# Block-diagonal products of a delta-rule scan: two half-array matmuls replaced by one matmul over the whole 128x128 array

## The chip, the cores and the metric

The kernel runs on one core of one Trainium2 chip. The metric is the device time of the whole program in microseconds (us), the median of several runs. TensorE has two lanes in the profile: PE is the matmul itself and PEld the load of its stationary operand (the weights). DVE is VectorE, ACT is ScalarE, POOL is GpSimd, SP issues the DMAs. TensorE's granted clock has two levels, 1.2 and 2.4 GHz; a granted clock of 0.92 over a stretch is a mixture of both.

## The reference, cut to what matters

One decoder layer over 2048 tokens: an RWKV-7 token mixer (12 heads of width 64) beside a 4-head cross-attention into 256 memory tokens, an output projection, and a squared-ReLU MLP of width 4096. What the change touches is this recurrence, and two small sums:

```python
def step(S, inp):                                   # one token, S is (heads, 64, 64)
    sa = einsum('bhvk,bhk->bhv', S, a_t)
    S = S * w_t + sa[..., None] * b_t + v_t[..., None] * k_t
    return S, einsum('bhvk,bhk->bhv', S, r_t)
bonus = sum(r_h * k_h * r_k, axis=-1) * v_h         # one number per token and head
q = rms_norm(q_mem)                                 # needs the sum of squares per token and head
```

The kernel computes the recurrence in chunks of 64 tokens. Within a chunk each head needs the inverse of a unit lower triangular 64x64 matrix; between chunks only S is carried.

## The kernel before, in words

**Stages.** First comes an input projection, `project(g)`, for four groups of 512 tokens; its matmuls are line 102 (`pz`). Then 16 pairs of chunks are worked through: `prepare(p)` builds everything of a pair that doesn't depend on S, `scan(d, S)` carries S through the pair's two chunks, and `post(p, ...)` normalises and gates the output. The projections of groups 1 to 3, the memory attention and the output projection (`output(g)`, line 629, `pout`) are spread between the pairs by `dense(...)`, as work for TensorE to do while the pairs wait for their small steps. At the end stands the MLP (lines 964 and 1073), which the change doesn't touch.

**Order.** A planner puts the instructions of each engine in an order, by priorities (`tc.cur_priority`) and by a simulated timeline. Each engine then runs its instructions strictly in that order. Buffers come from pools; a tile with `bufs=1` makes its next user wait until its last reader is done. All PSUM tiles of tag `z` (`psb`, `pb`, `pe`, `pe2`) share one buffer, and an engine that reads a PSUM tile and one that writes it take turns.

**The inverse.** Per chunk, twelve 64x64 matrices are inverted from 32x32 blocks. The two diagonal blocks of all heads come from a loop on DVE (lines 431 and 435) and arrive in the tile Z by DMA (line 447), head q=0 of a pair of heads in partitions 0 to 63 and head q=1 in 64 to 127, both in their own 64 columns; the rest of Z is zero. The off-diagonal block takes two products. Line 453 transposes the upper diagonal block on DVE into `te`. Line 459 multiplies it by the off-diagonal block of `PT`, one matmul per head with 32 weight columns and 32 moving columns, six heads of one q after the other, and line 461 copies the six results to `te2` on ACT. Line 466 multiplies `te2` (32 weight columns) by Z, again six heads at a time, and line 467 copies the six results on ACT into Z's off-diagonal block.

**Its use.** In `scan`, line 491 multiplies Z by the right side `rhs`: per pair of heads two matmuls, with 64 weight columns and 64 moving columns each. Around it, lines 485 (`prhs`) and 498 (`pS`) are products with 64 weight columns too.

**The small norms.** Line 405 (`psb`, for the bonus) and line 761 (`pq`, for the memory attention's query norm) multiply 128 tokens of a product by a matrix of two columns, 64 tokens at a time: 64 weight columns, 2 moving columns.

Each float32 matmul has two records in the profile, each with a weight load of its own. Twelve matmuls are so 24 records.

**Scratch.** `rows_norm` (line 150) writes a squared copy that nobody reads, `junk`, into a buffer of its own.

Of the kernel before, what the change touches and what calls it, by code (L numbers as in the profile page):

```python
# [9 lines left out]
F32 = mybir.dt.float32  # L10
# [9 lines left out]
P = 128  # L20
# [40 lines left out]
def hybrid_layer(  # L61
# [138 lines left out]
    def scan_setup():  # L200
        K["kkc"] = col(rw_k_k[0], "kkc")
        kac = col(rw_k_a[0], "kac")
        K["lbc"] = col(rw_lnx_b[0], "lbc")
        K["ka2"] = ka2 = cb.tile([P, NB], F32, name="ka2")
        nc.vector.tensor_scalar_mul(ka2, kac, 0.5)
        K["ka1"] = ka1 = cb.tile([P, NB], F32, name="ka1")
        nc.vector.tensor_scalar(ka1, kac, -0.5, 1.0, ALU.mult, ALU.add)
        K["lgr"] = lgr = cb.tile([P, MW], F32, name="lgr")
        nc.sync.dma_start(lgr, rw_lnx_g.to_broadcast([P, MW]))

        K["lora"], K["lob"] = [], []
        for which, (w2, w0) in enumerate(((rw_w2, rw_w0), (rw_a2, rw_a0))):
            src = pr.tile([P, MW], F32, tag="kk", name="lsrc")
            for o in range(2):
                nc.sync.dma_start(src[o * HD : (o + 1) * HD], w2[0])
            wt = cb.tile([P, MW], F32R, name=f"lora{which}")
            lo = pr.tile([P, MW], F32R, tag="EM", name="llo")
            nc.scalar.copy(wt[:HD], src[:HD])
            nc.scalar.copy(lo[HD:], src[HD:])
            nc.vector.tensor_tensor(wt[HD:], src[HD:], lo[HD:].bitcast(F32), op=ALU.subtract)  # L220
            K["lora"].append(wt)
            b0 = col(w0[0], f"lob{which}")
            nc.vector.tensor_scalar_mul(b0, b0, 0.5)
            K["lob"].append(b0)

        K["sel2"] = sel2 = cb.tile([96 + NH, MW], BF16, name="sel2")
        nc.gpsimd.memset(sel2, 0.0)
        for o in PARTS:
            so = sel2[o : o + NH]
            nc.gpsimd.memset(so, 1.0)  # L230
            nc.gpsimd.affine_select(so, so, pattern=[[1, MW]], compare_op=ALU.is_ge,
                                    fill=0.0, base=0, channel_multiplier=-HD)
            nc.gpsimd.affine_select(so, so, pattern=[[-1, MW]], compare_op=ALU.is_ge,
                                    fill=0.0, base=HD - 1, channel_multiplier=HD)
        K["rn3"] = rn3 = cb.tile([96 + NH, P], BF16, name="rn3")
        nc.gpsimd.memset(rn3, 0.0)
        K["g2s"] = g2s = cb.tile([P, MW], F32, name="g2s")
        nc.sync.dma_start(g2s, rw_g2[0])
        K["rkm"] = rkm = cb.tile([P, NB, 2], F32, name="rkm")
        nc.vector.memset(rkm, 0.0)  # L240
        rk_src = rw_r_k[0].rearrange("(b two) d -> two d b", two=2)
        nc.sync.dma_start(rkm[:HD, :, 0], rk_src[0])
        nc.sync.dma_start(rkm[HD:, :, 1], rk_src[1])

        K["sel1"] = sel1 = cb.tile([P, NB * NH], F32, name="sel1")
        nc.vector.memset(sel1, 0.0)
        nc.vector.memset(sel1[:HD, 0 : 14 * NB - 13 : 14], 1.0)
        nc.vector.memset(sel1[HD:, 1 : 14 * NB - 12 : 14], 1.0)

        K["msk"] = msk = cb.tile([P, P], F32, name="msk")  # L250
        nc.gpsimd.memset(msk, 1.0)
        nc.gpsimd.affine_select(msk[:HD, :C], msk[:HD, :C], pattern=[[1, C]], compare_op=ALU.is_ge,
                                fill=0.0, base=-1, channel_multiplier=-1)
        nc.gpsimd.affine_select(msk[:HD, C:], msk[:HD, C:], pattern=[[1, C]], compare_op=ALU.is_ge,
                                fill=0.0, base=0, channel_multiplier=-1)
        nc.sync.dma_start(msk[HD:], msk[:HD])
        K["rst"] = rst = cb.tile([P, 2 * P], F32, name="rst")
        nc.vector.memset(rst, 1.0)
        nc.vector.memset(rst.rearrange("p (a c) -> p a c", c=C)[:, :, 0], 0.0)

        zrow = K["zrow"] = dram.tile([2, 512], F32, name="zrow")
        ztmp = pr.tile([1, 512], F32, tag="zt", name="ztmp")
        for par in range(2):
            nc.vector.memset(ztmp, 0.0)
            nc.vector.memset(ztmp[:, par : 512 : 34], 1.0)
            nc.sync.dma_start(zrow[par : par + 1], ztmp)
        K["E"] = cb.tile([P, NB, 2, C + 1], F32, name="E")

        K["Z"] = [cb.tile([P, NB, 2 * C], F32, name=f"Z{i}") for i in range(3)]
        K["te2"] = [cb.tile([P, NB, 32], F32, name=f"te2{i}") for i in range(2)]  # L270
        nc.vector.memset(K["E"][:, :, :, 0], 1.0)
        for t in K["Z"] + K["te2"]:
            nc.gpsimd.memset(t, 0.0)
        S = st.tile([P, NB, HD], F32, tag="S", name="S")
        nc.vector.memset(S, 0.0)
        return S
# [4 lines left out]
    def prepare(p):  # L281
# [118 lines left out]
        nc.vector.tensor_tensor(kp, kp, R, op=ALU.mult)  # L400
        psb = psz.tile([P, NH], F32, tag="z", name="psb")
        for b in range(NB):
            for c in range(2):
                cc = slice(c * C, c * C + C)
                nc.tensor.matmul(psb[cc, 2 * b : 2 * b + 2], kp[:, b, cc], K["rkm"][:, b, :],
                                 start=True, stop=True)
        bs = pr.tile([P, NH], F32, name="bs", bufs=2)
        nc.scalar.copy(bs, psb)
        tc.cur_priority += UPS
# [32 lines left out]
        for c in range(2):  # L442
            d = ch[c]
            d["Z"] = Z = K["Z"][(2 * p + c) % 3]
            for q in range(2):
                for o in (q * C, q * C + 32):
                    nc.sync.dma_start(Z[o : o + 32, :, o : o + 32],
                                      zdr[o // 32 % 2, c, q * NB : (q + 1) * NB].rearrange("i s t -> s i t"))

            te = pr.tile([32, NH, 32], F32, name="te")  # L450
            te2 = K["te2"][c]
            for q in range(2):
                nc.vector.transpose(te[:, q * NB : (q + 1) * NB, :],
                                    Z[q * C : q * C + 32, :, q * C : q * C + 32])
            pe = psz.tile([P, NB, 32], F32, tag="z", name="pe")
            for q in range(2):
                lo = slice(q * C + 32, q * C + C)
                for b in range(NB):
                    nc.tensor.matmul(pe[lo, b, :], d["PT"][:32, q * NB + b, 32:C], te[:, q * NB + b, :],
                                     start=True, stop=True)  # L460
                nc.scalar.copy(te2[lo], pe[lo])
            pe = psz.tile([P, NB, 32], F32, tag="z", name="pe2")
            for q in range(2):
                hi, lo = slice(q * C, q * C + 32), slice(q * C + 32, q * C + C)
                for b in range(NB):
                    nc.tensor.matmul(pe[hi, b, :], te2[:, b, :], Z[:, b, lo], start=True, stop=True)
                nc.scalar.copy(Z[hi, :, lo], pe[hi])

            for q in range(2):
                nc.scalar.copy(d["PT"][:C, q * NB : (q + 1) * NB, :C], d["AR"][q * C : (q + 1) * C, :, :C])  # L470
        return dict(ch=ch, bs=bs)

    def scan(d, S):
        states = []
        for c in range(2):
# [11 lines left out]
            nc.scalar.copy(rhs, pc)  # L487
            pc = psc.tile([P, NB, HD], F32, tag="c", name="pw")
            for b in range(NB):
                for q in range(2):  # L490
                    nc.tensor.matmul(pc[q * C : (q + 1) * C, b, :], Z[:, b, q * C : (q + 1) * C], rhs[:, b, :],
                                     start=True, stop=True)
            for q in range(2):
                nc.scalar.copy(bycol(WV[:C])[:, q], pc[q * C : (q + 1) * C])
            pS = psc.tile([P, NB, HD], F32, tag="c", name="pS")
# [138 lines left out]
    def project(g):  # L634
        xh, xl = operands("xh"), operands("xl")
        for tt in range(4):
            tc.cur_priority -= UPX
            xt = ck.tile([P, D], F32, tag="PT", name="xt", bufs=4) if g == 0 else xrows("xt")
            r0 = g * G + tt * P
            nc.sync.dma_start(xt, x[r0 : r0 + P, :])  # L640
            rows_norm(xp, xt, xt, xp.tile([P, D], BF16, name="junk"))
            tsl = slice(tt * P, (tt + 1) * P)
            for _ in to_T(psx, "x", xt, halves(xh, xl, tsl)):
                tc.cur_priority += UPX
                yield
                tc.cur_priority -= UPX
            tc.cur_priority += UPX
# [63 lines left out]
    def memory_setup():  # L711
# [10 lines left out]
        for mb in range(2):  # L722
            mt = xrows("mt")
            nc.sync.dma_start(mt, mem[mb * P : (mb + 1) * P, :])
            rows_norm(xp, mt, mt, xp.tile([P, D], BF16, name="junk"))
            msl = slice(mb * P, (mb + 1) * P)
            yield from to_T(psx, "x", mt, [(mh[h][:, :, msl], ml[h][:, :, msl]) for h in range(2)])
        for part in range(2):
# [23 lines left out]
    def mem_attention(g, t0):  # L752
# [3 lines left out]
        nc.scalar.activation(qq, q2, AF.Square)  # L756
        pq = psx.tile([P, MH], F32, tag="x", name="pq")
        for b in range(2):
            for c in range(2):
                cc = slice(c * C, c * C + C)  # L760
                nc.tensor.matmul(pq[cc, 2 * b : 2 * b + 2], qq[:, b, cc], sel3, start=True, stop=True)
        yield
        qr = rsqrt_mean(xp, pq, MH, HD, RMS_EPS, "q")
        mxs = xp.tile([P, MH], F32, name="mxs")
# [376 lines left out]
```

## Time and profile before

| | |
|---|---|
| median of three runs | 2777.49 us (2774.64 to 2781.78) |
| the profiled execution's own time | 2781.47 us |
| its span, first to last instruction | 2779.8 us |
| mean granted TensorE clock | 0.956 |
| PE busy | 2620.1 us (94%), 17620 records |
| PEld busy | 2131.9 us (77%) |
| DVE busy | 1807.5 us (65%) |
| ACT busy | 1410.8 us (51%) |
| POOL busy | 413.1 us (15%) |

Busy time is the union of the durations of an engine's instructions. Matmuls are pipelined: one shows about 200 ns or more from start to end, and its successor starts long before that end. What a group of small matmuls costs TensorE is read from the starts: from the group's first start to the start of the next group. A shape such as "128*32 128x32 f32" means 128 rows and 32 weight columns of the array, and a moving operand of 32 columns; the load's own shape stands after PEld.

### The profile page before, as it was taken

How to read it: one execution, taken by the hardware profiler on the slowest of the kernel's cores; microseconds unless marked ns; L12 is line 12 of the kernel's file. 1: busy time of each engine (PE TensorE's matmuls, PEld its weight loads, DVE VectorE, ACT ScalarE, POOL GpSimd, SP SyncE). 2: the span in 40 equal slices, each digit the busy share in tenths (PEclk: the TensorE clock that was granted, in tenths of full speed). 3: DMA queues.
4: the chain of work that ended last, by engine and by line, in shares of the span. 5: the costliest groups of instructions: out<-in, count | busy, mean ns of one | idle time of the engine just before them, and what ended most of it. 6: DMA issues, size and time to landing. Idle time of an engine off the chain costs nothing.

```text
span 2779.8 us, 49460 instructions
## 1 busy us (share of the span) xinstructions
PE 2620.1 (94%) x17620; PEld 2131.9 (77%) x17620; DVE 1807.5 (65%) x4500; ACT 1410.8 (51%) x3053; POOL 413.1 (15%) x236
## 2 busy tenths in 40 slices
PE   6989999999899998997996999999999999999999
PEld 4777777777677777777885888878888888888887
DVE  4556657676866666778568777765875666655564
ACT  5564456465645547363446444444744444544443
POOL 2002133425304241333111000000100000000000
PEclk9999999999989988798997999999999999999999
DMA  8987564665454544335574576786775444456675
GB/s 251 286 263 215 166 176 135 168 174 165 135 152 138 144 126 120 100 86 164 160 241 133 201 260 244 275 306 191 246 258 170 145 144 155 150 192 208 211 252 167
DMA packets 468444, 519.35 MB, mean 187 GB/s; under 512 B 117538, under 2 KB 291682, under 8 KB 468196
## 3 DMA queue, kind: packets, MB, share of 16 engines
q1 hardware_dynamic: 468196, 516.18, 60.0%
q8 instruction: 139, 2.28, 0.3%
q14 instruction: 109, 0.89, 0.1%
HBM read 361.86 MB, written 154.14 MB: 186 GB/s over the span
## 4 chain that ended last, share of the span: by engine, by line
PE 74%; DMA 10%; DVE 9%; ACT 2%; issue 2%; SPq 2%; POOL 1%; DVEq 0%; ACTq 0%; POOLq 0%
PE pu L964 23%; PE py L1073 22%; PE pz L102 12%; PE pout L629 5%; PE pp L390 2%; DVE zt L431 1%; DVE Zw L435 1%; DMA zdr<-Zw 1%; PE prhs L485 1%; DMA qt<-q_d 1%; DMA KT<-rk_d 1%; DMA Z<-zdr 1%; DMA xt<-in_x_dram 1%; DMA ws<-in_rw_in_dram 1%; PE py L522 1%
## 5 line engine op out<-in xcount | busy, mean ns | idle before, releaser
L102 PE MATMUL pz<-xh,w 128*128 128x512 f32 x1408 | 484.9, 413 | 4.5 <-DVE last L681 2.7
L1073 PE MATMUL py<-wpl,hhh 128*128 128x512 f32 x896 | 349.3, 390 | 0.0
L1073 PE MATMUL py<-wph,hhl 128*128 128x512 f32 x896 | 348.3, 389 | 0.0
L1073 PE MATMUL py<-wph,hhh 128*128 128x512 f32 x896 | 344.0, 391 | 0.0
L102 PEld LDWEIGHTS pz<-xh,w 128*128 128x128 f32 x1408 | 268.9, 193 | 71.8 <-issue 6.6
L93 DVE TENSOR_TENSOR hhl<-hr,hhh 128x512 fp32r<-128x512 f32 x224 | 154.7, 691 | 225.6 <-ACT hhh L92 225.5
L92 ACT CAST hhh<-hr 128x512 fp32r<-128x512 f32 x224 | 139.1, 621 | 311.1 <-PE py L1073 295.5
L102 PE MATMUL pz<-xl,w 128*128 128x512 f32 x704 | 287.7, 409 | 0.4 <-DVE xl L93 0.4
L629 PE MATMUL pout<-wo,xh 128*128 128x256 f32 x1024 | 218.7, 307 | 18.9 <-DVE wo L93 9.6
L431 DVE TENSOR_TENSOR zt<-Ti,Zw 96x96 f32<-96x96 f32 (+20 forms) x736 | 171.2, 256 | 69.3 <-DMA Ti<-nd 49.7
L397 POOL TENSOR_TENSOR PT<-PT,msk 64x768 f32<-64x768 f32 x64 | 178.6, 2790 | 131.4 <-ACT PT L392 129.1
L629 PEld LDWEIGHTS pout<-wo,xh 128*128 128x128 f32 x1024 | 174.5, 205 | 28.9 <-DVE wo L93 12.3
L1073 PEld LDWEIGHTS py<-wph,hhl 128*128 128x128 f32 x896 | 168.4, 188 | 35.0
L1073 PEld LDWEIGHTS py<-wph,hhh 128*128 128x128 f32 x896 | 168.4, 188 | 34.8 <-DVE u L999 0.2
L1073 PEld LDWEIGHTS py<-wpl,hhh 128*128 128x128 f32 x896 | 168.4, 188 | 34.6
L435 DVE TENSOR_TENSOR Zw<-Zw,zt 96x96 f32<-96x96 f32 (+20 forms) x736 | 161.2, 242 | 6.7
L102 PEld LDWEIGHTS pz<-xl,w 128*128 128x128 f32 x704 | 135.8, 193 | 29.8 <-issue 1.9
L93 DVE TENSOR_TENSOR wpl<-wr,wph 128x512 fp32r<-128x512 f32 x224 | 153.3, 684 | 3.8 <-ACT wph L92 3.8
L629 PE MATMUL pout<-wo,xl 128*128 128x256 f32 x512 | 153.1, 299 | 0.0
L86 POOL TENSOR_TENSOR nr<-nm,nhalf 128x1 f32<-128x1 f32 x34 | 28.1, 827 | 789.2 <-DVE nm L84 736.3
L92 ACT CAST wph<-wr 128x512 fp32r<-128x512 f32 x224 | 138.2, 617 | 8.5 <-PE pu L964 7.5
L390 PE MATMUL pp<-AR,BK 64*128 64x128 f32 x768 | 94.5, 322 | 18.5 <-ACT PT L392 16.3
(293 smaller groups left out, 5640.5 us busy)
## 6 DMA issues: line engine op xcount, KB each, us to landing
w<-w_d SPq DMA_DIRECT2D x264, 256.0 KB, 4.0
hr<-hc_d SPq DMA_DIRECT2D x224, 256.0 KB, 2.8
ws<-in_w_ff_dram SPq DMA_DIRECT2D x32, 1024.0 KB, 5.7
hc_d<-hs SPq DMA_DIRECT2D x128, 256.0 KB, 2.2
wr<-t_d SPq DMA_DIRECT2D x128, 256.0 KB, 3.1
wr<-in_w_ff_dram SPq DMA_DIRECT2D x96, 256.0 KB, 3.0
w_d<-w SPq DMA_DIRECT2D x88, 256.0 KB, 4.2
ws<-in_w_out_dram SPq DMA_DIRECT2D x80, 256.0 KB, 4.3
```

The costliest lines, as they stand in the source:

```text
L86: nc.gpsimd.tensor_tensor(t1, t0, nhalf[: ssum.shape[0], :n], op=ALU.pow)
L92: nc.scalar.copy(hi, src)
L93: nc.vector.tensor_tensor(lo, src, hi.bitcast(F32), op=ALU.subtract)
L102: nc.tensor.matmul(ps, a(k), b(k), start=(k == 0 and i == 0), stop=(k == nk - 1 and i == 2))
L390: nc.tensor.matmul(pps[q][:, j, :], BK[c][rs, b, :], d["AR"][rs, b, :], start=True, stop=True)
L397: nc.gpsimd.tensor_tensor(PT[o : o + C, :, w:], PT[o : o + C, :, w:], K["msk"][o : o + C, w:].unsqueeze(1).to_broadcast([C, NH, 2 * C - w] ...
L431: nc.vector.tensor_tensor(zt[:, j0:j1, :nt], Ti[:, s, s + 1 :].unsqueeze(1).to_broadcast([96, j1 - j0, nt]), Zw[:, j0:j1, s : s + 1].to_br ...
L435: nc.vector.tensor_tensor(Zw[:, j0:j1, s + 1 :], Zw[:, j0:j1, s + 1 :], zt[:, j0:j1, :nt], op=ALU.add)
L485: nc.tensor.matmul(pc[rs, h // 2, :], PT[:, head(h), :C], WV[:, h * HD : (h + 1) * HD], start=True, stop=True)
L629: nc.tensor.matmul(po[:, t, :], a(k, t), w[k][:, b], start=(k == 0 and i == 0 and t == 0), stop=(k == KB - 1 and i == 2 and t == 1))
L964: nc.tensor.matmul(ps, a[u][:, k * P : (k + 1) * P], b[v][:, k, :], start=(first and k == 0 and i == 0), stop=(k == 3 and i == 2), skip_gr ...
L1073: nc.tensor.matmul(ps[bk], a[u][:, m * P : (m + 1) * P], b[v], start=(fresh and c == 0 and t == 0), stop=(c == NCH - 1 and t == 2), skip_g ...
```

## The change

Each pair of half-array products becomes one product over the whole array.

- `psb` and `pq`: the loop over the two halves of 64 tokens goes; one matmul has 128 weight columns and still 2 moving columns.
- `pw`: the loop over q goes; the whole 128x128 block diagonal of Z is the weight operand (128 columns), and the 64 moving columns stay.
- `pe`: the off-diagonal blocks of `PT` are first copied on ACT into a new zeroed tile `LB`, 128x128 per pair of heads (two copies per chunk). One matmul per pair then has LB as weights (128 columns) and `te` as moving operand (32 columns). `te` now lies in the partitions of its own head and is a zeroed tile that stays, as is `te2`, of which there is one instead of two.
- `pe2`: the operands change sides, so that Z is the weight operand (128 columns) and `te2` the moving one (32 columns). The result is the transpose of what it was; two DVE transposes from PSUM put it into Z, where two ACT copies did before.
- `junk` is taken from the ring of seven small tiles, `small`, where the projections' results and staged weights live; this makes room for `LB`.

```diff
-        K["te2"] = [cb.tile([P, NB, 32], F32, name=f"te2{i}") for i in range(2)]
+        K["LB"] = cb.tile([P, NB, P], F32, name="LB")
+        K["te"], K["te2"] = (cb.tile([P, NB, 32], F32, name=n) for n in ("te", "te2"))
...
-            for c in range(2):
-                cc = slice(c * C, c * C + C)
-                nc.tensor.matmul(psb[cc, 2 * b : 2 * b + 2], kp[:, b, cc], K["rkm"][:, b, :],
-                                 start=True, stop=True)
+            nc.tensor.matmul(psb[:, 2 * b : 2 * b + 2], kp[:, b, :], K["rkm"][:, b, :], start=True, stop=True)
...
-            te = pr.tile([32, NH, 32], F32, name="te")
-            te2 = K["te2"][c]
+            te, te2, LB = K["te"], K["te2"], K["LB"]
             for q in range(2):
-                nc.vector.transpose(te[:, q * NB : (q + 1) * NB, :],
-                                    Z[q * C : q * C + 32, :, q * C : q * C + 32])
+                hi, lo = slice(q * C, q * C + 32), slice(q * C + 32, q * C + C)
+                nc.vector.transpose(te[hi], Z[hi, :, hi])
+                nc.scalar.copy(LB[hi, :, lo], d["PT"][:32, q * NB : (q + 1) * NB, 32:C])
             pe = psz.tile([P, NB, 32], F32, tag="z", name="pe")
+            for b in range(NB):
+                nc.tensor.matmul(pe[:, b, :], LB[:, b, :], te[:, b, :], start=True, stop=True)
             for q in range(2):
                 lo = slice(q * C + 32, q * C + C)
-                for b in range(NB):
-                    nc.tensor.matmul(pe[lo, b, :], d["PT"][:32, q * NB + b, 32:C], te[:, q * NB + b, :],
-                                     start=True, stop=True)
                 nc.scalar.copy(te2[lo], pe[lo])
             pe = psz.tile([P, NB, 32], F32, tag="z", name="pe2")
+            for b in range(NB):
+                nc.tensor.matmul(pe[:, b, :], Z[:, b, :], te2[:, b, :], start=True, stop=True)
             for q in range(2):
                 hi, lo = slice(q * C, q * C + 32), slice(q * C + 32, q * C + C)
-                for b in range(NB):
-                    nc.tensor.matmul(pe[hi, b, :], te2[:, b, :], Z[:, b, lo], start=True, stop=True)
-                nc.scalar.copy(Z[hi, :, lo], pe[hi])
+                nc.vector.transpose(Z[hi, :, lo], pe[lo])
...
             for b in range(NB):
-                for q in range(2):
-                    nc.tensor.matmul(pc[q * C : (q + 1) * C, b, :], Z[:, b, q * C : (q + 1) * C], rhs[:, b, :],
-                                     start=True, stop=True)
+                nc.tensor.matmul(pc[:, b, :], Z[:, b, :], rhs[:, b, :], start=True, stop=True)
...
-            rows_norm(xp, xt, xt, xp.tile([P, D], BF16, name="junk"))
+            rows_norm(xp, xt, xt, small([P, D], "junk", BF16))
...
-            for c in range(2):
-                cc = slice(c * C, c * C + C)
-                nc.tensor.matmul(pq[cc, 2 * b : 2 * b + 2], qq[:, b, cc], sel3, start=True, stop=True)
+            nc.tensor.matmul(pq[:, 2 * b : 2 * b + 2], qq[:, b, :], sel3, start=True, stop=True)
```

## Rows read from the trace of the kernel before

**Rows 1.** The page's busy time: engine, busy us, share of the span, records.

```profile
PE 2620.1 (94%) x17620; PEld 2131.9 (77%) x17620; DVE 1807.5 (65%) x4500; ACT 1410.8 (51%) x3053; POOL 413.1 (15%) x236
```

**Rows 2.** Busy us (instructions) by stretch, granted clock, DMA share, GB/s.

```profile
1100.00:1200.00 100.00, 93.78 (x867) 78.92 (x865) 76.93 (x272) 46.81 (x127) 25.21 (x12) 0.81 0.33 90
...
200.00:1420.00 1220.00, 1137.95 (x10927) 918.16 (x10927) 824.50 (x2777) 638.52 (x1606) 378.07 (x187) 0.92 0.53 149
...
1530.00:2780.00 1250.00, 1240.54 (x5410) 1010.63 (x5409) 799.89 (x1266) 591.24 (x1013) 7.26 (x6) 1.00 0.63 210
```

**Rows 3.** The chain that ended last, share of the span by engine.

```profile
PE 74%; DMA 10%; DVE 9%; ACT 2%; issue 2%; SPq 2%; POOL 1%; DVEq 0%; ACTq 0%; POOLq 0%
```

**Rows 4.** PE's waits from 200 to 1420: us in total, times, longest.

```profile
PE pe L459 <- ACT te L461: 5.6, 4, 2.0
...
PE pe L459 <- DVE te L453: 3.7, 5, 1.3
```

**Rows 5.** Weight loads of four lines: ns min/median/max, first and last start, shape.

```profile
L301 PEld LDWEIGHTS pss<-sq,sel x192: 88/93/144, 138.6 to 1243.9; 128*12 128x12 f32 x192
...
L459 PEld LDWEIGHTS pe<-te,PT x768: 101/108/153, 282.4 to 1360.8; 32*32 32x32 f32 x192
...
L405 PEld LDWEIGHTS psb<-rkm,th x384: 132/138/227, 219.1 to 1330.6; 128*64 128x64 f32 x192
...
L563 PEld LDWEIGHTS pg<-SG,g2s x192: 186/192/338, 364.8 to 1419.0; 128*128 128x128 f32 x192
```

**Rows 6.** PE's groups in order of time: start us, length us, line, shape, records.

```profile
580.63 0.40 PE L761 MATMUL pq<-sel,qt 128*64 128x2 f32 x8
580.96 0.51 PE L102 MATMUL pz<-xh,w 128*128 128x512 f32 x1
...
609.09 0.39 PE L102 MATMUL pz<-xl,w 128*128 128x512 f32 x1
609.33 0.63 PE L102 MATMUL pz<-xh,w 128*128 128x512 f32 x2
609.80 0.40 PE L102 MATMUL pz<-xl,w 128*128 128x512 f32 x1
610.12 0.56 PE L459 MATMUL pe<-te,PT 32*32 32x32 f32 x12
610.62 0.72 PE L102 MATMUL pz<-xh,w 128*128 128x512 f32 x2
...
615.67 0.56 PE L459 MATMUL pe<-te,PT 32*32 32x32 f32 x12
...
627.22 0.56 PE L466 MATMUL pe<-Z,te 128*32 128x32 f32 x12
627.71 0.33 PE L491 MATMUL pw<-rhs,Z 128*64 128x64 f32 x2
...
634.36 0.94 PE L563 MATMUL pg<-SG,g2s 128*128 128x128 f32 x6
635.23 0.80 PE L491 MATMUL pw<-rhs,Z 128*64 128x64 f32 x18
...
1009.09 0.87 PE L405 MATMUL psb<-rkm,th 128*64 128x2 f32 x24
1009.81 0.90 PE L491 MATMUL pw<-rhs,Z 128*64 128x64 f32 x24
1010.64 0.44 PE L522 MATMUL py<-S,AR 64*64 64x64 f32 x6
```

**Rows 7.** DVE and ACT lines: count, busy us, mean ns, idle before, releasers.

```profile
L453 DVE STREAM_TRANSPOSE te<-Z 32x192 f32<-32x192 f32 x64 | 23.4, 365 | 70.1 <-DMA Z<-zdr 51.6 <-PE pe L459 17.7
L461 ACT COPY te<-pe 32x192 f32<-32x192 f32 x64 | 19.9, 311 | 35.7 <-PE pe L459 34.7
L467 ACT COPY Z<-pe 32x192 f32<-32x192 f32 x64 | 19.7, 308 | 29.4 <-PE pe L466 28.2 <-PE pss L301 0.4
...
L150 ACT ACTIVATE junk<-xt 128x1024 bf16<-128x1024 f32 x16 | 16.8, 1053 | 18.6 <-DMA xt<-in_x_dram 17.0 <-DVE th L365 1.3 <-DVE nm L84 0.2
```

More of the change, by code (lines that the diff above doesn't have):

```diff
@@ L269, in scan_setup @@
         K["Z"] = [cb.tile([P, NB, 2 * C], F32, name=f"Z{i}") for i in range(3)]
-        K["te2"] = [cb.tile([P, NB, 32], F32, name=f"te2{i}") for i in range(2)]
+        K["LB"] = cb.tile([P, NB, P], F32, name="LB")
+        K["te"], K["te2"] = (cb.tile([P, NB, 32], F32, name=n) for n in ("te", "te2"))
         nc.vector.memset(K["E"][:, :, :, 0], 1.0)
-        for t in K["Z"] + K["te2"]:
+        for t in K["Z"] + [K["LB"], K["te"], K["te2"]]:
             nc.gpsimd.memset(t, 0.0)
@@ L724, in memory_setup @@
             nc.sync.dma_start(mt, mem[mb * P : (mb + 1) * P, :])
-            rows_norm(xp, mt, mt, xp.tile([P, D], BF16, name="junk"))
+            rows_norm(xp, mt, mt, small([P, D], "junk", BF16))
             msl = slice(mb * P, (mb + 1) * P)
```

## The prediction

> **What bounds the kernel now.** I read the page's busy times first: PE is busy 94% of the span, the next engine 65% [rows 1]. An average hides stages, so the busy time by stretch comes next [rows 2]. In the MLP, from 1530 us on, PE is busy 1240.5 of 1250 us; the change has nothing there. Everything that it touches lies between 200 and 1420 us, where PE is busy 1138 of 1220 us (93%), DVE 824 and ACT 639, at a granted clock of 0.92. The chain that ended last is PE for 74% of the span [rows 3]. The MLP's 1250 us are 45 of these points, so about 29 points, 806 us, lie in the first 1530 us: a little over half of that time the end is set by TensorE's work, the rest by small steps and DMAs. The stage is thus mostly, not wholly, paid in TensorE time, and 82 us of PE idle are there to take some in. So the question is what a group of small products occupies, read from start to start, and not how many instructions it has.
>
> **What the old groups occupy.** Starts in [rows 6], at the full clock:
> - `pe`: 12 records from 610.12 to 610.62, 0.50 us; two groups a chunk, 32 chunks: 32.0 us.
> - `pe2`: 12 records from 627.22 to 627.71, 0.49 us; 64 groups: 31.4 us.
> - `pw`: 24 records from 1009.81 to 1010.64, 0.83 us; 32 chunks: 26.6 us.
> - `psb`: 24 records from 1009.09 to 1009.81, 0.72 us; 16 pairs: 11.5 us.
> - `pq`: 8 records from 580.63 to 580.96, 0.33 us; 16 times: 5.3 us.
>
> Together 106.8 us. A change of array shape costs something besides: in a run of `pz` the starts lie 0.235 us apart (609.09 to 609.80 is three), but 0.32 us when `pe` follows (609.80 to 610.12). That is 0.09 us on entry. Some 190 old groups make 17 us of it. The exit is inside the figures above.
>
> **What the new ones will occupy.** All have a weight operand of 128 columns. The trace has no float32 record with 128 weight columns and few moving ones, so I bound it. The loads of the trace last 93 ns at 12 columns, 108 at 32, 138 at 64 and 192 at 128 [rows 5]: (192 - 93) / 116 = 0.85 ns a column, on a fixed part that overlaps with neighbours. At that slope 128 columns hold the load path 0.11 us a record. The nearest whole row is `pg`, the only repeated float32 group that fills the array: 6 records from 634.36 to 635.23, 0.145 us each with a change of shape behind them, or 0.11 each if that change is 0.2. `psb` says that the load sets the pace: its records move only 2 columns, yet each half of the array takes 12 records in 0.72 us, 0.060 each, against 0.042 for `pe`, which moves 32 columns and loads 32. The lower end is what half-array records cost on average now, 0.028 us (0.67 us of 24 if `psb`'s switch is 0.05). The upper end is a load that doesn't hide behind the matmul before it, 0.11 plus 0.85 ns x 64 = 0.16 us. I take 0.11, `pg`'s price, because the loads are the same size.
>
> Per group of 12 records that is 1.32 us, for `pq`'s 4 records 0.44. Three groups a chunk: 96 x 1.32 = 126.7; `psb` 16 x 1.32 = 21.1; `pq` 16 x 0.44 = 7.0; together 154.9 us, so 48 us more than before. Halving the records saves nothing, since the weight columns stay (`pw`, `psb`, `pq`: 2 x 64 against 128) or double (`pe`, `pe2`: 2 x 32 against 128), and two column halves no longer load side by side. New groups have the projections' shape and switch only next to the scan's own half-array products; if half of 128 groups switch, in and out at 0.1 us each, 13 us come back of the 17 that go. TensorE's balance: 48 + 13 - 17 = +44 us, between -71 (at 0.028: 40 us of groups) and +84 (the fourth rival below).
>
> **How much of it reaches the end.** Of +44 us, PE's 7% idle takes some. The chain says a little over half, the busy share says nine tenths; I take 0.7: +31 us.
>
> **Other edits.**
> - Before, `pe` of one q waited for the ACT copy of the other, as both sit in one PSUM tile: PE stood 5.6 us for it [rows 4]. The two turns become one: -4 us, between -6 and 0. Next in line is the DVE transpose (3.7 us), which stays.
> - DVE gets 64 transposes out of PSUM. None is in the trace; the same shape from SBUF takes 0.365 us, an ACT copy out of PSUM 0.308 [rows 7]. I take 0.365: 23 us more on an engine that is busy 68% of the stretch and 9% of the chain. In its queue the scan's state update and the inversion loop stand behind it. +3 us, between 0 and 23.
> - ACT loses 64 copies at 0.308 us and gains 64 of the same size into `LB`, taken at 0.311: nothing. `LB`, `te` and `te2` are single, so the second chunk's copy waits for the first chunk's `pe`; behind a waiting copy stand all PSUM evictions in ACT's queue. ACT already waits 34.7 us for `pe` before its `te2` copies, off the chain mostly. 0, at worst +15.
> - `junk` from the ring of seven: 18 squares of 1.05 us on ACT [rows 7] must now find a slot that a projection result has left. The covered time is the lead by which a group's rows are normalised ahead of its matmuls. 0; without the cover a group's start slips, at worst what these squares already wait for x, 17 us.
> - Two more memsets on POOL at setup, before its first use at 282 us: nothing. No DMA is added, and nothing is moved past a queue.
> - The clock: one hundredth over the stretch is worth about 12 us, and 1100 to 1200 ran at 0.81 with PE 94% busy [rows 2]. I see no reason for a sign: 0, between -15 and +20.
>
> Sum against the profiled execution: 2781.5 + 31 - 4 + 3 = 2811.5 us. The median of the runs is 4.0 us under that execution, so the forecast in that measure is 2807 us, 1.1% slower. Its own range is 2787 to 2835.
>
> **Rivals.**
> 1. *A record costs the same whatever its columns.* 24 records of `psb` in about 0.7 us and 12 of `pe` in 0.5 are 0.03 to 0.04 us each, for quite different shapes; so one may read it as a price per instruction. Then 1408 records go at 0.028: 40 us of groups, -71 x 0.7 - 1 = -51, 2727 us. Against it stand the load durations of [rows 5] and `pg`. The Trainium skill, "TensorEngine Tiling (Array Packing)", section Instruction Overhead, gives some 60 cycles to every matmul and tells not to tile a dimension that is small already; that is this rival. Chance 0.10.
> 2. *The turns between engines count more than TensorE's time.* Today a chunk's block takes four turns (PE, ACT, PE, ACT, twice), and they stand far apart in PE's order: `pe` at 610.12 and 615.67, the last `pe2` at 627.22. Two turns fewer per chunk save some 10 us of latency. Where the stage is paced by the inverse's arrival, the end comes earlier even though PE does more, at the best until PE has no idle: 82 - 44 = 38 us; half of it is 2758 us. For it: only half of the chain is PE. Against it: PE waits only 9.3 us for these products in all [rows 4]. It decides when the wait for `Z` or `te`, not `pout` and `pz`, ends PE's idle. Chance 0.14.
> 3. *All of it falls into idle time.* +44 us into 82 us: 2777 us. Chance 0.13.
> 4. *The load doesn't hide.* At 0.16 us for `pw` and 0.137 for `pe` and `pe2`, the groups take about 195 us, +84 with the switches, 0.8 of it on the path: 2843 us. The same comes of a clock that falls as in 1100 to 1200. Chance 0.13.
>
> **How the numbers follow.** The forecast has 0.50. A measurement of this kernel tells about 0.3% (8 us) from no change. Faster: rivals 1 and 2, 0.24. Within 0.3%: 0.13. Slower: 0.63. The range takes in rivals 2 to 4 and leaves rival 1 and the far end of 4 out: 2750 to 2850.
>
> **What would show it.** Right: starts of `pw`, `psb`, `pe` groups about 1.3 us apart for 12 records, all near 0.11 us a record, equal for 2, 32 and 64 moving columns; loads of 192 ns; PE busier by 30 to 45 us between 200 and 1450 us; the MLP as long as before but starting later. Wrong: 12 records in 0.4 us or less; or groups at 1.3 us with the MLP starting no later, and PE's idle gone.

## The result, and the profile after

| | before | after |
|---|---|---|
| median | 2776.84 us (2774.64 to 2781.78) | 2872.84 us (2871.66 to 2873.35) |
| ratio, 95% interval | | 1.0343, 1.0325 to 1.0360 |
| span of the profiled execution | 2779.8 us | 2871.1 us |
| mean granted clock | 0.956 | 0.941 |
| records on PE | 17620 | 16212 |

The change costs 96 us, 3.4%. The forecast was 2807 us, slower, with 2850 as its upper end: the sign was right, the size three times too small, and the time lies outside the range.

The busy times of the changed kernel: engine, busy us, share, records. PE has 1408 records less than in [rows 1] and is busy 63 us longer.

```profile
PE 2683.6 (93%) x16212; PEld 2213.4 (77%) x16212; DVE 1831.2 (64%) x4564; ACT 1405.3 (49%) x3053; POOL 410.7 (14%) x237
```

The same by stretch, cut at the first matmul of the MLP. Columns: stretch, length, busy us (instructions) of PE, PEld, DVE, ACT, POOL, granted clock, DMA share, GB/s. First the kernel before:

```profile
0.00:1518.00 1518.00, 1369.19 (x12180) 1113.45 (x12180) 996.31 (x3217) 810.23 (x2024) 402.95 (x229) 0.92 0.58 169
1518.00:2780.00 1262.00, 1250.95 (x5440) 1018.46 (x5440) 811.18 (x1283) 600.56 (x1030) 10.16 (x8) 0.99 0.63 208
```

Then the changed one:

```profile
0.00:1601.00 1601.00, 1430.05 (x10772) 1196.05 (x10772) 1021.57 (x3281) 810.61 (x2024) 400.50 (x230) 0.90 0.55 160
1601.00:2871.00 1270.00, 1253.51 (x5440) 1017.30 (x5440) 809.61 (x1283) 594.73 (x1031) 10.23 (x8) 0.99 0.63 207
```

The MLP starts 83 us later and is 8 us longer. In the 83 us PE is busy 61 us more and idle 22 us more, and the granted clock of the stretch is lower. Over the whole span the time at the lower level (1.2 GHz) is twice the missing share: 2 x 0.044 x 2780 = 245 us before, 2 x 0.059 x 2871 = 339 us after.

Groups of the changed kernel on PE, start and length in us, to be read from start to start as in [rows 6]:

```profile
615.31 1.52 PE L463 MATMUL pe<-te,Z 128*128 128x32 f32 x12
616.67 0.48 PE L102 MATMUL pz<-xh,w 128*128 128x512 f32 x1
...
632.36 1.40 PE L405 MATMUL psb<-rkm,th 128*128 128x2 f32 x12
633.62 0.52 PE L553 MATMUL pty<-ident,yc 128*128 128x128 f32 x3
...
644.65 1.45 PE L489 MATMUL pw<-rhs,Z 128*128 128x64 f32 x12
645.94 0.28 PE L417 MATMUL pb<-ident,BK 128*128 128x128 f32 x1
```

Twelve records take 1.36, 1.26 and 1.29 us with 32, 2 and 64 moving columns: one price, whatever the moving columns. Their loads last what `pg`'s do in [rows 5] (ns min/median/max):

```profile
L405 PEld LDWEIGHTS psb<-rkm,th x192: 186/192/337, 219.4 to 1377.4; 128*128 128x128 f32 x192
```

### The profile page after: what moved, and what is told of

Its sections match the earlier page's. It is cut to its first block, busy times and chain, and to the rows that moved or that the text cites. A ratio compares the mean times of both kernels' runs of the same rounds, so it can differ in the third digit from the quotient of the medians.

```text
span 2871.1 us, 46779 instructions
## 1 busy us (share of the span) xinstructions
PE 2683.6 (93%) x16212; PEld 2213.4 (77%) x16212; DVE 1831.2 (64%) x4564; ACT 1405.3 (49%) x3053; POOL 410.7 (14%) x237
## 4 chain that ended last, share of the span: by engine, by line
PE 60%; DVE 8%; DMA 6%; ACT 4%; issue 3%; POOL 1%; SPq 1%; DVEq 0%; POOLq 0%; ACTq 0%
PE py L1068 21%; PE pu L959 17%; PE pz L102 6%; PE pout L626 5%; DMA ws<-in_w_ff_dram 2%; DVE zt L430 1%; DVE Zw L434 1%; PE pe L456 1%; DMA wt<-in_w_ff_dram 1%; PE pw L489 1%; PE pp L392 1%; PE pe L463 1%; POOL PT L399 1%; PE prhs L484 1%; DMA zdr<-Zw 1%
## 5 line engine op out<-in xcount | busy, mean ns | idle before, releaser
L102 PE MATMUL pz<-xh,w 128*128 128x512 f32 x1408 | 499.2, 423 | 2.7 <-DVE xl L93 0.9
L102 PEld LDWEIGHTS pz<-xh,w 128*128 128x128 f32 x1408 | 277.0, 199 | 72.0 <-issue 8.5
L102 PE MATMUL pz<-xl,w 128*128 128x512 f32 x704 | 294.9, 419 | 0.6 <-DVE xl L93 0.6
L626 PE MATMUL pout<-wo,xh 128*128 128x256 f32 x1024 | 209.5, 301 | 18.9 <-ACT wo L92 11.9
L86 POOL TENSOR_TENSOR nr<-nm,nhalf 128x1 f32<-128x1 f32 x34 | 34.2, 1005 | 810.9 <-DVE nm L84 785.1
L673 DVE SCALAR_TENSOR_TENSOR sl<-pz,muc,sl 128x511 f32<-128x511 f32 x80 | 59.8, 747 | 79.6 <-ACT sl L672 79.1
```

The costliest lines, as they stand in the source:

```text
L86: nc.gpsimd.tensor_tensor(t1, t0, nhalf[: ssum.shape[0], :n], op=ALU.pow)
L102: nc.tensor.matmul(ps, a(k), b(k), start=(k == 0 and i == 0), stop=(k == nk - 1 and i == 2))
L626: nc.tensor.matmul(po[:, t, :], a(k, t), w[k][:, b], start=(k == 0 and i == 0 and t == 0), stop=(k == KB - 1 and i == 2 and t == 1))
L673: nc.vector.scalar_tensor_tensor(sl[:, 1:], pz[:, : G - 1], mu, sl[:, 1:], ALU.mult, ALU.add)
```

## The experiments

Two theories stood at the start. W: the width of the weight load is the cost, with the clock that falls with it. R: the other edits are, the single buffers, the DVE transposes and the ring. Each ratio is against runs of the kernel before on the same chip.

**halves.** The changed kernel with each whole-array product in two column halves:

```diff
-                nc.tensor.matmul(pe[:, b, :], LB[:, b, :], te[:, b, :], start=True, stop=True)
+                for q in range(2):
+                    qs = slice(q * C, (q + 1) * C)
+                    nc.tensor.matmul(pe[qs, b, :], LB[:, b, qs], te[:, b, :], start=True, stop=True)
```

> The changed kernel, with each of its whole-array products issued as two products of 64 weight columns, one for each half of the output; LB, te, te2, the transposes on DVE and the junk slot stay as changed. Theory W (the width of the weight load: 0.112 us a record instead of half of that, and the clock that falls with it): a group of 12 pairs costs about 0.7 us again, and the time returns to 2765 to 2800 us. Rival R (the other edits: single buffers, transposes on DVE, the ring): it stays at 2850 to 2875 us.

Measured: 2825.7 us, ratio 1.0173 (1.0144 to 1.0202). Neither range holds it: half of the loss goes with the width, half stays. The granted clock stays low as well: 0.940 to 0.945 in the four runs, against 0.940 to 0.942 in the changed kernel's. A group of 24 records takes 0.82 us:

```profile
633.50 0.89 PE L470 MATMUL pe<-te,Z 128*64 128x32 f32 x24
634.32 0.94 PE L569 MATMUL pg<-SG,g2s 128*128 128x128 f32 x6
```

**junk_only.** The kernel before with one edit (and the same for the memory's rows):

```diff
-            rows_norm(xp, xt, xt, xp.tile([P, D], BF16, name="junk"))
+            rows_norm(xp, xt, xt, small([P, D], "junk", BF16))
```

> The kernel before with junk alone taken from the ring of seven. Theory W: 2777 us within 10. Rival R: if the ring holds the projection back, 2795 us or more, with the end of the projections later than 1051 us.

Measured: 2795.6 us, ratio 1.0054 (1.0034 to 1.0074); W missed it, R just holds, and its second sign came too: the last projection matmul starts at 1083 us. ACT in the kernel before, two of the four squares of group 3, some 290 us before its projection starts at 728.93:

```profile
428.30 1.05 ACT L150 ACTIVATE junk<-xt 128x1024 bf16<-128x1024 f32 x1
...
437.62 1.05 ACT L150 ACTIVATE junk<-xt 128x1024 bf16<-128x1024 f32 x1
```

ACT in junk_only: all four come at the last moment.

```profile
732.79 1.11 ACT L150 ACTIVATE junk<-xt 128x1024 bf16<-128x1024 f32 x1
...
736.61 1.05 ACT L150 ACTIVATE junk<-xt 128x1024 bf16<-128x1024 f32 x1
...
744.75 1.09 ACT L150 ACTIVATE junk<-xt 128x1024 bf16<-128x1024 f32 x1
...
749.53 1.06 ACT L150 ACTIVATE junk<-xt 128x1024 bf16<-128x1024 f32 x1
```

PE in junk_only between the last projection matmul of group 2 and the first of group 3:

```profile
726.45 0.39 PE L102 MATMUL pz<-xh,w 128*128 128x512 f32 x1
737.10 1.04 PE L160 MATMUL pt<-ident,xt 128*128 128x128 f32 x8
...
763.92 0.79 PE L102 MATMUL pz<-xh,w 128*128 128x512 f32 x1
```

PE in the kernel before, at the same place:

```profile
699.78 0.39 PE L102 MATMUL pz<-xh,w 128*128 128x512 f32 x1
700.47 0.66 PE L160 MATMUL pt<-ident,xt 128*128 128x128 f32 x4
...
728.93 0.47 PE L102 MATMUL pz<-xh,w 128*128 128x512 f32 x1
```

37 us without a projection matmul against 29: the transposes start 11 us after the last projection matmul instead of 1, since the rows are not ready. Over the starts of groups 1 to 3 these stretches sum to 100 us against 74. In the kernel's code a slot of the ring is free again only when its last reader is done; the trace shows the late squares, not which slot they waited for.

**pw_norms.** The kernel before with these lines alone (and psb, pq likewise):

```diff
-                for q in range(2):
-                    nc.tensor.matmul(pc[q * C : (q + 1) * C, b, :], Z[:, b, q * C : (q + 1) * C], rhs[:, b, :],
-                                     start=True, stop=True)
+                nc.tensor.matmul(pc[:, b, :], Z[:, b, :], rhs[:, b, :], start=True, stop=True)
```

> The kernel before with pw, psb and pq alone over the whole array; the inverse as before, no new tile. Theory W: TensorE does 32 x 0.65 + 16 x 0.6 + 16 x 0.11 = 32 us more, so 2805 to 2830 us (the upper end if the clock falls with it). Rival R: 2777 us within 10, since none of its edits is in it.

Measured: 2800.9 us, ratio 1.0080 (1.0053 to 1.0106). Slower without any new tile or copy, as W has it; its size, 22 us, is under W's range. The range was set too high: by the rows above, the groups grow by 32 x (1.29 - 0.83) + 16 x (1.26 - 0.72) and a little for `pq`, some 25 us, not 32.

**offdiag.** The changed kernel with pw, psb and pq back in halves (the edit above, reversed).

> The changed kernel with pw, psb and pq in halves as before: only the two products of the off-diagonal block and what belongs to them are changed. Theory W: 64 x (1.34 - 0.5) = 54 us less the switches of shape, about 45 us more on TensorE at most, 2805 to 2840 us; this and pw_norms add up to the change's 96 us. Rival R: 2860 to 2875 us, all of the loss.

Measured: 2864.0 us, ratio 1.0309 (1.0269 to 1.0349), 85 us. W's range missed it; R's holds it, though R alone can't be right either, as pw_norms loses 22 us. The two parts make 107 us where the whole change makes 96.

**halves_own.** The run halves with `junk` in a buffer of its own, one byte an element (and `saturate=False` on the square that writes it):

```diff
-            rows_norm(xp, xt, xt, small([P, D], "junk", BF16))
+            rows_norm(xp, xt, xt, xp.tile([P, D], mybir.dt.float8e4, name="junk"))
```

> The run halves with junk in a buffer of its own again (written in one byte an element, so that it fits). If the ring's cost stands beside the others: 2825 - 15 = 2810 us within 8, and the squares of groups 1 to 3 start ahead of the projection's end again, as before. If it is hidden behind them: 2825 us within 8.

Measured: 2797.3 us, ratio 1.0062 (1.0039 to 1.0086). The ring costs 28 us here, more than expected, and stands beside the rest. Half of the squares of groups 1 to 3 have their lead back (52.1 to 445.8 us), as expected. With the same records on TensorE the mean clock of the runs is 0.952 instead of 0.942.

**after_own.** The changed kernel with the same edit.

> The changed kernel with junk in a buffer of its own again (one byte an element, so that it fits). The ring cost 16 us on the kernel before and 28 us in halves; here 2872 - 16 to 28 = 2844 to 2856 us if it stands beside the wide loads. If the ring is hidden behind them: 2865 us or more.

Measured: 2860.3 us, ratio 1.0310 (1.0281 to 1.0339). The time lies between the two ranges: the ring costs 13 us of the change, and as the intervals of the two ratios overlap, that is hardly clear of the noise. With these runs the loss is a sum: 2778.6 before, +19 for the new inverse in halves (2797.3), +63 for the whole-array width (2860.3), +13 for the ring (2872.8). The terms depend on the order. With the ring in place, from halves to the changed kernel, the width costs 47 us, and the ring then 28.

**fill_load and fill_move.** The kernel before, with two kinds of extra work ahead of `pw`, nearly equal in TensorE time; both results are overwritten.

```diff
+            for b in range(NB):                       # fill_load
+                nc.tensor.matmul(pc[:, b, :2], ident, rhs[:, b, :2], start=True, stop=True)
...
+            for b in range(4):                        # fill_move
+                nc.tensor.matmul(pc[:, :3, :], ident, rhs[:, :3, :], start=True, stop=True)
```

> The kernel before with six more float32 matmuls per chunk ahead of pw, over the whole array, 128 weight columns and 2 moving columns, their result overwritten: 32 x 12 x 0.112 = 43 us more of TensorE, set by weight loads. Theory L (records that load much and move little lower the granted clock): 2840 us or more, the time at the lower clock up by 60 us or more, clearly more than in fill_move. Rival A (any 43 us more of TensorE in this stage cost about that and some idle): 2805 to 2830 us, like fill_move within 10 us.

> The kernel before with four more float32 matmuls per chunk ahead of pw, 128 weight columns and 192 moving columns: 32 x 8 x 0.165 = 42 us more of TensorE, set by the moving columns. Theory L: 2800 to 2820 us with no more time at the lower clock than before, 20 us or more under fill_load. Rival A: 2805 to 2830 us, like fill_load within 10 us.

Measured: fill_load 2842.5 us, ratio 1.0237 (1.0192 to 1.0282); fill_move 2814.3 us, ratio 1.0135 (1.0115 to 1.0155). A group of fill_load, from 594.17 to 595.60:

```profile
594.17 1.50 PE L490 MATMUL pw<-rhs,ident 128*128 128x2 f32 x12
595.60 0.92 PE L493 MATMUL pw<-rhs,Z 128*64 128x64 f32 x24
```

One of fill_move, from 603.93 to 605.43, is no shorter:

```profile
603.93 1.57 PE L490 MATMUL pw<-rhs,ident 128*128 128x192 f32 x8
605.43 0.92 PE L493 MATMUL pw<-rhs,Z 128*64 128x64 f32 x24
```

Before the MLP, fill_load:

```profile
0.00:1592.00 1592.00, 1448.55 (x12565) 1187.53 (x12565) 982.60 (x3217) 813.05 (x2024) 391.36 (x229) 0.90 0.56 161
```

and fill_move:

```profile
0.00:1556.00 1556.00, 1406.44 (x12437) 1145.75 (x12438) 1002.18 (x3217) 810.86 (x2024) 397.96 (x229) 0.94 0.58 165
```

PE is idle 143 and 150 us, so the sum of the waits doesn't make the difference. PE is busy 42 us longer where the extra records load, at a clock of 0.90 against 0.94; the medians are 28 us apart. All four runs of each agree: 0.941 to 0.950 and 0.959 to 0.963. The granted clock of fill_move lies even above that of the kernel before (0.92). In fill_load the clock also falls to the lower level while PE has no idle time, here behind a group of line 490, and the next 24 records take 1.48 us instead of the 0.83 of [rows 6]:

```profile
653.91 1.40 PE L490 MATMUL pw<-rhs,ident 128*128 128x2 f32 x12
655.24 1.55 PE L493 MATMUL pw<-rhs,Z 128*64 128x64 f32 x24
656.72 1.03 PE L301 MATMUL pss<-sq,sel 128*12 128x128 f32 x4
```

The same stretch, ahead of the fall and behind it:

```profile
651.00:655.00 4.00, 4.00 (x53) 3.34 (x48) 4.00 (x28) 2.13 (x5) 0.00 (x0) 1.00 0.79 237
655.50:658.50 3.00, 3.00 (x32) 2.33 (x31) 2.97 (x18) 1.54 (x4) 0.00 (x0) 0.50 0.01 3
```

Before the MLP, 12 of the 33 falls of fill_load come without idle time of PE in the last 2 us ahead of them, and 1 of the 23 of fill_move. Theory L's ranges hold; rival A had the two within 10 us of each other.

**after_wide.** The changed kernel with more moving columns; the surplus is overwritten by the next product.

```diff
-                nc.tensor.matmul(pc[:, b, :], Z[:, b, :], rhs[:, b, :], start=True, stop=True)
+                n = min(2, NB - b)      # 4 for pe and pe2
+                nc.tensor.matmul(pc[:, b : b + n, :], Z[:, b, :], rhs[:, b : b + n, :], start=True, stop=True)
```

> The changed kernel with more moving columns: pe and pe2 move up to 128 columns instead of 32 and pw 128 instead of 64; what falls outside a pair's own columns is overwritten by the next product. The load of 128 columns (0.112 us a record) should hide it, so TensorE's groups are no longer. Theory L (records that load much and move little lower the granted clock): the time at the lower clock falls by 60 us or more from 340, and the kernel is faster than the changed one, 2835 to 2860 us, though it streams more. Rival A (the clock falls with the idle gaps and not with the kind of record): 2865 us or more, the time at the lower clock as before.

Measured: 2846.0 us, ratio 1.0249 (1.0217 to 1.0281), 27 us faster than the changed kernel, though up to four times the columns go through. The groups are no longer than before, 1.26 us:

```profile
609.66 1.42 PE L465 MATMUL pe<-te,Z 128*128 128x128 f32 x12
610.92 0.48 PE L102 MATMUL pz<-xh,w 128*128 128x512 f32 x1
```

The clock of the stretch is 0.93 instead of 0.90, with PE idle 191 us instead of 171, so the sum of the idle gaps is not what lowered it. Over the span of the profiled execution, 2 x 0.043 x 2842 = 244 us are at the lower level, as in the kernel before. The other three runs have a lower clock, and over all four the mean is 266 us:

```profile
0.00:1576.00 1576.00, 1385.39 (x10772) 1153.47 (x10772) 1034.44 (x3281) 811.08 (x2023) 400.39 (x230) 0.93 0.56 163
```

**dve_evac.** The kernel before with pe2's sides swapped and DVE in ACT's place:

```diff
-                    nc.tensor.matmul(pe[hi, b, :], te2[:, b, :], Z[:, b, lo], start=True, stop=True)
-                nc.scalar.copy(Z[hi, :, lo], pe[hi])
+                    nc.tensor.matmul(pe[lo, b, :], Z[:, b, lo], te2[:, b, :], start=True, stop=True)
+                nc.vector.transpose(Z[hi, :, lo], pe[lo])
```

> The kernel before with only the sides of pe2's product swapped, 32 weight and 32 moving columns as before, so that a DVE transpose puts the result into Z where an ACT copy did. If the move to DVE carries the 31 us that halves loses beyond junk: 2795 to 2815 us. If the single buffers and copies of LB, te and te2 do: 2777 us within 8.

Measured: 2775.2 us, ratio 0.9995 (0.9979 to 1.0012): no difference. The 24 us of transposes on DVE are hidden.

**halves_pool.** halves_own with the copies into LB on POOL:

```diff
-                nc.scalar.copy(LB[hi, :, lo], d["PT"][:32, q * NB : (q + 1) * NB, 32:C])
+                nc.gpsimd.tensor_copy(LB[hi, :, lo], d["PT"][:32, q * NB : (q + 1) * NB, 32:C])
```

> The run halves_own with the two copies into LB on POOL instead of ACT. In halves_own ACT stood 40.8 us ahead of these copies until the chunk before had used LB up. If that wait, with everything behind it in ACT's queue, is what remains of the loss (19 us): 2778 to 2786 us. If it lies off the path: 2797 us within 8.

Measured: 2812.6 us, ratio 1.0127 (1.0093 to 1.0160): 15 us slower, outside both ranges. In halves_own ACT waits for the chunk before to release LB (us, times, longest):

```profile
ACT LB L456 <- PE pe L461: 40.8, 19, 11.5
```

In halves_pool POOL waits four times as long, with the masks of `PT` and the output's scaling behind it in its queue:

```profile
POOL LB L456 <- PE pe L461: 167.0, 16, 35.5
```

The run shows what the wait costs in POOL's queue, between masks of 2.8 us each, and not what it costs in ACT's. How much of the 19 us it makes stays open; a second LB was not tried.

**turns.** The kernel before with both heads' twelve matmuls in one alternating group, both copies behind it; `pe2` likewise:

```diff
-            for q in range(2):
-                lo = slice(q * C + 32, q * C + C)
-                for b in range(NB):
-                    nc.tensor.matmul(pe[lo, b, :], d["PT"][:32, q * NB + b, 32:C], te[:, q * NB + b, :],
-                                     start=True, stop=True)
-                nc.scalar.copy(te2[lo], pe[lo])
+            for b in range(NB):
+                for q in range(2):
+                    lo = slice(q * C + 32, q * C + C)
+                    nc.tensor.matmul(pe[lo, b, :], d["PT"][:32, q * NB + b, 32:C], te[:, q * NB + b, :],
+                                     start=True, stop=True)
+            for q in range(2):
+                lo = slice(q * C + 32, q * C + C)
+                nc.scalar.copy(te2[lo], pe[lo])
```

> The kernel before with pe's and pe2's twelve matmuls each issued in one group, the two heads of a pair alternating, and both copies behind them: 32 weight columns and every tile as before. Theory W (TensorE's time is what a pair of column halves takes side by side): 24 records in 0.4 to 0.75 us instead of twice 0.5, 8 to 19 us less on TensorE per product, together 16 to 38 us, so 2745 to 2768 us. Rival T (the end is set by waits, and turns between PE and ACT are what counts): also faster, but with the groups no shorter. If two column quarters don't load side by side: 2777 us within 8.

Measured: 2761.6 us, ratio 0.9939 (0.9921 to 0.9957): faster than both kernels. 24 records now take the 0.50 us that 12 took in [rows 6]; the outputs of the two heads that alternate lie in different columns of the array:

```profile
633.70 0.57 PE L459 MATMUL pe<-te,PT 32*32 32x32 f32 x24
634.20 0.92 PE L495 MATMUL pw<-rhs,Z 128*64 128x64 f32 x24
```

## Why the prediction was wrong, point by point

**The price of the groups: right.** Forecast were 1.32 us for 12 records and 155 us in all. By the rows above it is 64 x 1.36 + 32 x 1.29 + 16 x 1.26 + 16 x 0.45 (`pq`, whose rows aren't shown: 0.36 to 0.52) = 156 us. Of the signs named, the groups, the loads and the later start of the MLP came; PE is busier by 61 us before the MLP instead of 30 to 45; 49 are the groups, and the rest fits the lower clock. The Trainium skill, "TensorEngine Tiling (Array Packing)", section Instruction Overhead, gives each matmul some 60 cycles of overhead, so that 1 moving column takes as long as 60. The trace agrees as far as few moving columns go, with 1.26 us for 2 and 1.36 for 32. Read as one price per record, as in rival 1, it fails: `psb` moves 2 columns before and after, and 12 records with wide loads take 1.26 us where 24 with narrow ones took 0.72 [rows 6].

**How much of it reaches the end: 0.7, not shown wrong.** From halves to the changed kernel the groups grow by 64 x (1.36 - 0.82) + 32 x (1.29 - 0.83) + 16 x (1.26 - 0.72) + 16 x (0.45 - 0.33) = 60 us at nearly the same clock (means of the runs 0.942 and 0.941), and 47 us arrive, 0.8 of it. From halves_own to after_own the same 60 us bring 63, but there the clock falls too, from 0.952 to 0.941. In fill_move 36 to 38 us arrive of at most 48, at a better clock.

**The clock: wrong, the first step that failed.** I wrote 0, between -15 and +20, and saw no reason for a sign. It has one: in the changed kernel the time at the lower level is 339 us instead of 245. As a group takes nearly twice as long there, the 94 us more are worth up to 47 us (an estimate from these two figures). From halves_own to after_own, where only the width changes, the runs' mean clocks and spans give 266 and 338 us, worth up to 36 of the 63 us that arrive. after_wide gets 27 us back by moving more columns at the same price, and fill_load loses 28 us against fill_move. The width is not the only thing that lowers the clock. halves has the records of halves_own, and with the ring it is at 328 us; width and ring together give 340, hardly more than either alone. In the changed kernel 29 of the 34 falls before the MLP also come with some idle time of PE in the last 2 us ahead of them. The forecast's own fourth rival named a falling clock, but only as a chance, at 0.13.

**The ring for junk: wrong, the second step.** I named the cover, the lead by which a group's rows are normalised, and priced it at 0 with 17 us at worst. The lead is gone in junk_only, and the ring costs 17 us on the kernel before, 28 in halves and some 13 in the changed kernel. There the way is less plain: the three stretches without projection matmuls sum to 90 us with the ring and to 101 without it.

**Fewer turns, -4 us: not seen.** Before `pe`, the wait for ACT's `te` copies ([rows 4]) is gone, but a longer one has come in its place, for the DVE transposes, 3.7 us before (us, times, longest):

```profile
PE pe L456 <- DVE te L452: 18.7, 7, 6.5
```

turns has that wait too (16.4 us) and is faster than the kernel before. It shows that fewer turns and alternating columns are worth 17 us where neither LB nor wide loads come with them; how much of that the turns alone make was not separated.

**DVE transposes, +3 us: right within the measurement.** dve_evac is 0.9995 of the kernel before; one transpose out of PSUM takes 380 ns:

```profile
L466 DVE STREAM_TRANSPOSE Z<-pe 32x192 f32<-32x192 f32 x64 | 24.3, 380 | 58.1 <-PE pe L463 57.1
```

**The rest of the new inverse: wrong, the third step, cause open.** The forecast had -1 us for it, with the single LB at 0 and at worst +15. halves_own loses 19 us although its groups are shorter than before (64 x 0.82 = 52 against 63 us). dve_evac clears the DVE transposes; the single LB, `te` and `te2`, the copies into LB and the turns were not told apart.

So of the 96 us the forecast had 30. The width was sized at 31 us and costs 63 with the clock that falls with it; the ring was set to nothing and costs about 13; the rest of the new inverse was set to -1 and costs 19.

## What to carry to other kernels

For small float32 products look at the weight columns that load one behind the other, not at the number of matmuls: two half-array products in different columns took 0.72 us where one over the whole array took 1.26 (`psb`), and alternating between columns let two groups pass in the time of one. Look at the granted clock beside the group's time. Here records with wide loads and few moving columns went with a lower clock, and more moving columns in the same time made the kernel faster. When an edit puts a scratch tile into a ring that others use, ask whose lead it ends.

## What the runs showed of the hardware that I had not expected

Two kinds of extra work for TensorE went with different clocks: with nearly equal group times (1.43 and 1.50 us a chunk) and nearly equal idle, 128-column loads with 2 moving columns ran at 0.90 before the MLP and 192 moving columns at 0.94. In after_wide more moving columns in the same slots went with 0.93 instead of 0.90. Matmuls with 32 weight columns whose outputs lie in different columns of the array run side by side when they alternate: 24 records in the 0.50 us of 12.
